# Two attentions of a hybrid decoder layer in one sequence of half-array passages

## The chip, the cores and the metric

The kernel runs on one core of a Trainium2 chip. The core has a matmul engine, TensorE (PE in the profile, with its weight loads in a lane of their own, PEld), a vector engine (VectorE, DVE), an activation engine (ScalarE, ACT), GpSimd (POOL) and SyncE (SP), whose queue issues nearly all transfers here. The metric is the time of one execution on the device in microseconds, less is better.

## The reference

Two decoder layers work on 256 tokens of width 1024. The input projection of a layer feeds three groups of heads; cut to what the change touches:

```python
proj = h @ w_in
q_r = rotary(split_heads(rq, RET_HEADS)); k_r = rotary(split_heads(rk, RET_HEADS)) * scale
y_ret = merge_heads(head_group_norm(retention(q_r, k_r, v_r))) * jax.nn.silu(rg)
y_moba = merge_heads(moba_attention(mq, mk, mv, rel_bias))     # causal softmax with a relative bias
y_conv = cb * causal_dwconv(cc * ch, conv_w)
mix = concatenate([y_ret, y_moba, y_conv], -1) @ w_out
x = layer_norm(DN_ALPHA * x + mix); x = layer_norm(DN_ALPHA * x + conv_ffn(x))
```

Six heads of 64 features do retention, six do MoBA attention, which at 256 tokens has one block and so is plain causal softmax attention. Retention weights the scores by a fixed decay per head, has no softmax, and is normalised per head behind its values.

## The kernel before

All weights are split into a rounded part and a remainder (`whi`, `wlo`, by ACT and DVE in `split`, lines 82 and 83), and most products are made of three matmuls, high by high, high by low and low by high. Tokens are two tiles of 128, and the features of two heads share the 128 partitions of one tile.

In each layer, ahead of the stretch that changes, PE makes the MoBA queries and keys (`feature_block`, lines 307 to 309). Then comes the stretch itself. Twelve projection blocks (retention queries and keys, `rq` and `rk`, three each, then six blocks of the short convolution) run through a generator, `projections`, and each is yielded in two halves of 12 full-array matmuls of 256 columns (lines 396 to 398). I call such a half a slice; `fill(n)` runs n of them. Between the slices the attentions are put by hand, one pair of heads at a time:

- `moba_scores(j)`: four products per head, one in plain fp32 and three of split parts, each head on one half of the 128 rows of the array (`Pair.scores`, line 335, the halves in `HALVES`). DVE adds the bias and takes the row minimum of the negated scores (445), ACT the exponential (447), DVE the reciprocal and the scaling (450, 452).
- `moba_transpose(j)`: six full-array transposes (459); ACT copies them back to SBUF (460).
- `moba_values(j)`: four products with 64 stationary columns, one head on each half of the columns (467); ACT and DVE split the result into `cath` and `catl`.
- `retention_scores(j)`: the same product as for MoBA (335); DVE multiplies by the decay (492, 493) into `rs`.
- `retention_values(h)`: three products per head with 128 queries as stationary columns and 64 features streamed (498 to 500), into the two banks `po`.

A plain fp32 matmul of the program shows as two matmuls and two weight loads in the trace. PE takes its work in the program's order. The loops put two or one slices between any two of these passages (`FILL`), so that scores wait through five slices for their transposes. All PSUM tiles come from two pools of four banks: `acc`, for the projections, and `att`, for the attentions, of which `po` holds two from the first retention scores to the head normalisation. The order on DVE and ACT is made by a scheduler when the program is built. SP fetches weights five blocks ahead.

```python
for i in range(NH // 2 + 2):
    if i < NH // 2: moba_scores(i)
    fill(FILL[0])
    if 0 <= i - 1 < NH // 2: moba_transpose(i - 1)
    fill(FILL[1])
    if 0 <= i - 2 < NH // 2: moba_values(i - 2)
```

Of the kernel before, what the change touches and what calls it, by code (L numbers as in the profile page):

```python
# [12 lines left out]
AF = mybir.ActivationFunctionType  # L13
# [3 lines left out]
P = 128  # L17
D = 1024
T = 256
# [3 lines left out]
NH = 6  # L23
# [17 lines left out]
TAIL = 4  # L41
LAST = 5
GSTEP = 3
FILL = (2, 1, 1, 2)
AT = ((7, 8), (7, 8), (6, 8), (13, 15))
WARM = 6
BIAS_AT = 6
# [1 line left out]
HALVES = (slice(0, HD), slice(HD, P))  # L49
# [3 lines left out]
def hybrid_decoder(ctx: ExitStack, tc: tile.TileContext, x, xw, wva, wvb, wf, wt, w_out, wg, w_up, w_down,  # L53
                   conv_w, ffn_w, ln1_g, ln1_b, ln2_g, ln2_b, rel_bias,
                   c_ident, c_rot, c_decay, c_bucket, out):
    nc = tc.nc
# [9 lines left out]
    def acc():  # L66
        return pa.tile([P, 512], F32, name="acc", tag="acc")

    def att():
        return pb.tile([P, 512], F32, name="att", tag="att")  # L70
# [10 lines left out]
    def split(dst_hi, dst_lo, src):  # L81
        nc.scalar.copy(dst_hi, src)  # L82
        nc.vector.tensor_sub(dst_lo, src, dst_hi.bitcast(F32))  # L83
# [141 lines left out]
    def mirrored(src, n):  # L225

        return bass.AP(tensor=src.tensor, offset=src.offset + P - 1, ap=[list(src.ap[0]), [P, n], [-1, P]])
# [31 lines left out]
    def fetch_table(func, after):  # L259

        nc.scalar.activation(sp.tile([P, 1], F32, name="table", tag="table", bufs=1), after[:, :1], func)
# [11 lines left out]
    for k in range(KD):  # L273
        hi, lo = weights(0, "v", k)
        for g in (1, 0):
            n, c = VG[g][1] - VG[g][0], slice(0, T) if g else slice(T, 3 * T)
# [12 lines left out]
    for l in range(DEPTH):  # L289
# [25 lines left out]
        rv = [v[:, HW:2 * HW] for v in vt]  # L315
# [21 lines left out]
        def buf256(name):  # L337
            return ap.tile([P, T], F32, name=name, tag="b256", bufs=3)

        moba = [Pair() for _ in range(3)]  # L340
        for i, m in enumerate(moba):
            p = feature_block(f"mq{i}")[:, :T]
            q = buf256("q")
# [86 lines left out]
        def fill(n):  # L430
            for _ in range(n):
                next(bulk, None)
# [3 lines left out]
        prob = {}  # L436

        def moba_scores(j):
            banks = [att(), att()]
            moba[j].scores(banks, slice(0, P), slice(P, 3 * P))  # L440
            for h, ps in zip((2 * j, 2 * j + 1), banks):
                m = sp.tile([P, 4], F32, name="sm", tag="sm")
                pr_ = prob[h] = ap.tile([P, HW], F32, name="prob", tag="t384", bufs=6)
                for t, s, bs in ((0, slice(0, P), slice(P, T)), (1, slice(P, 3 * P), slice(0, T))):
                    nc.vector.tensor_tensor_reduce(pr_[:, s], ps[:, s], bias[:, h, bs], -1.0, 3e38,
                                                   op0=ALU.add, op1=ALU.min, accum_out=m[:, t:t + 1])
                    nc.scalar.activation(pr_[:, s], pr_[:, s], AF.Exp, bias=m[:, t:t + 1], scale=-1.0,
                                         accum_out=m[:, 2 + t:3 + t])
                rs = sp.tile([P, 2], F32, name="rs", tag="rs")
                nc.vector.reciprocal(rs, m[:, 2:4])  # L450
                for t, s in ((0, slice(0, P)), (1, slice(P, 3 * P))):
                    nc.vector.tensor_scalar_mul(pr_[:, s], pr_[:, s], rs[:, t:t + 1])

        def moba_transpose(j):

            for h in (2 * j, 2 * j + 1):
                pt = att()
                for i in range(3):
                    nc.tensor.transpose(pt[:, i * P:i * P + P], prob[h][:, i * P:i * P + P], ident)
                nc.scalar.copy(prob[h].rearrange("p (t q) -> p t q", t=3), mirrored(pt[:, :HW], 3))  # L460

        def moba_values(j):

            po = att()
            for t, s in ((0, slice(0, T)), (1, slice(T, 3 * P))):
                for h, r in zip((2 * j, 2 * j + 1), HALVES):
                    nc.tensor.matmul(po[r, t * P:T], mv[t][:, h * HD:h * HD + HD], prob[h][:, s],
                                     start=t == 0, stop=t == 1)
            split(ch[:, 3 + j, :], cl[:, 3 + j, :], po[:, :T])

        for i in range(NH // 2 + 2):
            if i < NH // 2:
                moba_scores(i)
            fill(FILL[0])
            if 0 <= i - 1 < NH // 2:
                moba_transpose(i - 1)
            fill(FILL[1])
            if 0 <= i - 2 < NH // 2:
                moba_values(i - 2)

        fetch_table(AF.Silu, prob[NH - 1])


        po = [att(), att()]
        rs_ = {}

        def retention_scores(j):
            banks = [att(), att()]
            ret[j].scores(banks, slice(T, 3 * P), slice(0, T))
            for h, ps in zip((2 * j, 2 * j + 1), banks):  # L490
                s = rs_[h] = ap.tile([P, HW], F32, name="rs", tag="t384", bufs=6)
                nc.vector.tensor_mul(s[:, 0:T], ps[:, 0:T], decay[:, h, :])
                nc.vector.tensor_mul(s[:, T:3 * P], ps[:, T:3 * P], decay[:, h, 0:P])

        def retention_values(h):
            s = rs_[h]
            c = slice(h * HD, h * HD + HD)
            nc.tensor.matmul(po[0][:, c], s[:, 0:P], rv[0][:, c], start=True, stop=True)
            nc.tensor.matmul(po[1][:, c], s[:, P:T], rv[0][:, c], start=True, stop=False)
            nc.tensor.matmul(po[1][:, c], s[:, T:3 * P], rv[1][:, c], start=False, stop=True)  # L500

        for j in range(NH // 2 + 1):
            if j < NH // 2:
                while len(turned) <= j:
                    next(bulk)
                if j == 0:
                    fill(FILL[2])
                retention_scores(j)
            fill(FILL[3])
            if j:  # L510
                retention_values(2 * j - 2)
                retention_values(2 * j - 1)
        mvr = sp.tile([P, NT * NH, 2], F32, name="gmv", tag="gmv", bufs=1)
        for t in range(NT):
            st = sp.tile([P, NH, 6], F32, name="gst", tag="gst", bufs=2)
# [12 lines left out]
        for t, p in enumerate(token_group("rg")):  # L528
            c, g = slice(t * HW, t * HW + HW), slice(t * NH, t * NH + NH)
# [254 lines left out]
```

## Time and profile before

| | |
|---|---|
| median of 3 runs | 625.51 us (624.73 to 625.52) |
| the profiled execution | 625.28 us |
| its span, first to last instruction | 623.2 us |
| PE busy | 611.4 us, 98% |
| DVE busy | 456.9 us, 73% |
| ACT busy | 351.5 us, 56% |
| the stretch of the attentions, layer 0 and 1 | 49.31 and 48.93 us |

A row of the timeline gives the start and the time of one instruction, or of several of one kind in a row (x4). A matmul's time there includes its way through the array, so matmuls that follow each other overlap: their pace is the distance between starts. A passage's price is read as the distance from the matmul ahead of it to the one behind it.

### The profile page before, as it was taken

Reading aid. Unit: us, or ns where it says so; the run is one execution under the profiler, and the core shown is the slowest. Engines: PE = TensorE matmul, PEld = TensorE weight load, DVE = VectorE, ACT = ScalarE, POOL = GpSimd, SP = SyncE. Lnnn points to the kernel's source line nnn. Section 1 sums busy time; section 2 is a strip of 40 time slices with the busy share of each in tenths; the row PEclk is TensorE's granted clock in tenths of the full one; section 3 lists DMA queues with packets and bytes.
Section 4 is the critical chain, followed back from the end, with each engine's and each line's share of the span. In section 5 each row is a group of like instructions: output and inputs, shape, how many; then the busy total and the mean of one; then the engine's idle time right before and its main releaser. Section 6 shows DMA issues by size and latency. Waiting matters only on the chain.

```text
span 623.2 us, 10002 instructions
## 1 busy us (share of the span) xinstructions
PE 611.4 (98%) x3774; PEld 540.7 (87%) x3774; DVE 456.9 (73%) x834; ACT 351.5 (56%) x637; POOL 17.0 (3%) x18
## 2 busy tenths in 40 slices
PE   8999999999999999999999999999999999999994
PEld 6899998788888888899889999987888888888993
DVE  6478889777676777678765778888867676767846
ACT  6579837256556565566346794461655656556620
POOL 0100002000000000000000000101000000000001
PEclk9999999999999999999999999999999999999998
DMA  8987355546566556668327435473655555566501
GB/s 311 351 295 239 120 169 187 218 150 214 180 192 190 185 186 191 197 214 293 108 92 265 150 93 173 160 254 105 226 179 191 185 187 182 199 193 176 172 2 67
DMA packets 33675, 115.92 MB, mean 186 GB/s; under 512 B 3957, under 2 KB 4764, under 8 KB 33628
## 3 DMA queue, kind: packets, MB, share of 16 engines
q1 hardware_dynamic: 33356, 114.50, 56.3%
q0 software_dynamic: 272, 0.80, 0.4%
q8 instruction: 29, 0.48, 0.3%
q14 instruction: 18, 0.15, 0.1%
HBM read 114.22 MB, written 1.06 MB: 185 GB/s over the span
## 4 chain that ended last, share of the span: by engine, by line
PE 93%; DVE 4%; DMA 1%; POOL 0%; issue 0%; ACT 0%; SPq 0%; DVEq 0%; POOLq 0%
PE acc L632 18%; PE acc L633 9%; PE att L230 6%; PE att L231 6%; PE att L232 6%; PE acc L231 5%; PE acc L232 5%; PE acc L230 5%; PE acc L308 5%; PE acc L309 5%; PE acc L307 5%; PE acc L396 5%; PE acc L397 4%; PE acc L398 4%; PE att L335 2%; DVE st L240 1%
## 5 line engine op out<-in xcount | busy, mean ns | idle before, releaser
L83 DVE TENSOR_TENSOR wlo<-raw,whi 128x1024 fp32r<-128x1024 f32 (+3 forms) x207 | 229.5, 1115 | 87.5 <-ACT whi L82 86.6
L82 ACT CAST whi<-raw 128x1024 fp32r<-128x1024 f32 (+3 forms) x207 | 197.8, 963 | 114.0 <-PE acc L632 41.9
L632 PE MATMUL acc<-xx,whi 128*128 128x512 f32 x480 | 170.8, 398 | 0.0
L633 PE MATMUL acc<-xx,wlo 128*128 128x256 f32 x480 | 134.7, 281 | 0.0
L632 PEld LDWEIGHTS acc<-xx,whi 128*128 128x128 f32 x480 | 90.2, 188 | 22.0
L633 PEld LDWEIGHTS acc<-xx,wlo 128*128 128x128 f32 x480 | 90.6, 189 | 1.3
L308 PE MATMUL acc<-xx,whi 128*128 128x256 f32 x240 | 67.9, 283 | 0.0
L309 PE MATMUL acc<-xx,wlo 128*128 128x256 f32 x240 | 67.9, 283 | 0.0
L307 PE MATMUL acc<-xx,whi 128*128 128x256 f32 x240 | 67.9, 283 | 0.0
L396 PE MATMUL acc<-xx,whi 128*128 128x256 f32 x208 | 61.4, 295 | 0.0
L397 PE MATMUL acc<-xx,whi 128*128 128x256 f32 x208 | 58.7, 282 | 0.0
L398 PE MATMUL acc<-xx,wlo 128*128 128x256 f32 x208 | 58.7, 282 | 0.0
L231 PE MATMUL att<-whi,hl 128*128 128x512 f32 x144 | 56.5, 392 | 0.0
L232 PE MATMUL att<-wlo,hh 128*128 128x512 f32 x144 | 56.0, 389 | 0.0
L230 PE MATMUL att<-whi,hh 128*128 128x512 f32 x144 | 55.7, 394 | 0.0
L230 PE MATMUL acc<-whi,xx 128*128 128x512 f32 (+2 forms) x128 | 45.8, 362 | 1.5 <-ACT whi L82 1.5
L308 PEld LDWEIGHTS acc<-xx,whi 128*128 128x128 f32 x240 | 46.1, 192 | 0.2
L307 PEld LDWEIGHTS acc<-xx,whi 128*128 128x128 f32 x240 | 46.1, 192 | 0.2
L309 PEld LDWEIGHTS acc<-xx,wlo 128*128 128x128 f32 x240 | 46.1, 192 | 0.0
L231 PE MATMUL acc<-whi,xx 128*128 128x512 f32 (+2 forms) x128 | 44.9, 352 | 0.8 <-DVE xx L83 0.8
L232 PE MATMUL acc<-wlo,xx 128*128 128x512 f32 (+2 forms) x128 | 44.3, 350 | 0.0
L396 PEld LDWEIGHTS acc<-xx,whi 128*128 128x128 f32 x208 | 39.6, 190 | 2.7 <-issue 1.0
(141 smaller groups left out, 953.9 us busy)
## 6 DMA issues: line engine op xcount, KB each, us to landing
raw<-in_w_up_dram SPq DMA_DIRECT2D x80, 512.0 KB, 4.3
raw<-in_w_down_dram SPq DMA_DIRECT2D x44, 512.0 KB, 4.3
raw<-in_wf_dram SPq DMA_DIRECT2D x36, 512.0 KB, 4.6
raw<-in_w_out_dram SPq DMA_DIRECT2D x16, 512.0 KB, 3.4
raw<-in_wg_dram SPq DMA_DIRECT2D x8, 512.0 KB, 4.4
raw<-in_xw_dram SPq DMA_DIRECT2D x7, 512.0 KB, 5.7
raw<-in_wt_dram SPq DMA_DIRECT2D x8, 384.0 KB, 3.3
lnp<-in_ln_g_dram SPq DMA_DIRECT2D x4, 512.0 KB, 3.9
```

The lines of the kernel that those rows point to most:

```text
L82: nc.scalar.copy(dst_hi, src)
L83: nc.vector.tensor_sub(dst_lo, src, dst_hi.bitcast(F32))
L230: nc.tensor.matmul(ps, lhi, rhi, start=first, stop=False)
L231: nc.tensor.matmul(ps, llo, rhi, start=False, stop=False)
L232: nc.tensor.matmul(ps, lhi, rlo, start=False, stop=last)
L307: nc.tensor.matmul(ps[:, :T], hi[:, c], xh[:, k, :], start=k == 0, stop=False)
L308: nc.tensor.matmul(ps[:, :T], hi[:, c], xl[:, k, :], start=False, stop=False)
L309: nc.tensor.matmul(ps[:, :T], lo[:, c], xh[:, k, :], start=False, stop=k == KD - 1)
L396: nc.tensor.matmul(ps[:, :T], hi[:, c], xh[:, k, :], start=k == 0, stop=False)
L397: nc.tensor.matmul(ps[:, :T], hi[:, c], xl[:, k, :], start=False, stop=False)
L632: nc.tensor.matmul(ps, hi[:, c], xx[:, k].rearrange("p s t -> p (s t)"), start=k == 0, stop=False)
L633: nc.tensor.matmul(ps[:, T:], lo[:, c], xx[:, k, 0, :], start=False, stop=k == KD - 1)
```

## The change

The MoBA loop and the retention loop become one loop of five rounds. In a round the values of one pair, the scores of another, and in the last two rounds retention scores, stand directly behind each other; then come the transposes of the pair before, and then four slices. The retention values come after the loop, all six heads in one block, and the last four slices behind them. Their stationary columns are taken in halves of 64 queries, each on one half of the array's columns. `po` is allocated behind the loop, the MoBA values take an `acc` bank instead of an `att` bank, and ACT's table for Silu is fetched one round earlier.

```diff
-FILL = (2, 1, 1, 2)
+FILL = 4
...
         def moba_values(j):
 
-            po = att()
+            po = acc()
...
-        for i in range(NH // 2 + 2):
-            if i < NH // 2:
-                moba_scores(i)
-            fill(FILL[0])
-            if 0 <= i - 1 < NH // 2:
-                moba_transpose(i - 1)
-            fill(FILL[1])
-            if 0 <= i - 2 < NH // 2:
-                moba_values(i - 2)
-
-        fetch_table(AF.Silu, prob[NH - 1])
-
-
-        po = [att(), att()]
+
         rs_ = {}
...
         def retention_values(h):
+
             s = rs_[h]
             c = slice(h * HD, h * HD + HD)
-            nc.tensor.matmul(po[0][:, c], s[:, 0:P], rv[0][:, c], start=True, stop=True)
-            nc.tensor.matmul(po[1][:, c], s[:, P:T], rv[0][:, c], start=True, stop=False)
-            nc.tensor.matmul(po[1][:, c], s[:, T:3 * P], rv[1][:, c], start=False, stop=True)
-
-        for j in range(NH // 2 + 1):
-            if j < NH // 2:
+            for t, k, q in ((0, 0, 0), (1, 0, P), (1, 1, T)):
+                for r in HALVES:
+                    nc.tensor.matmul(po[t][r, c], s[:, q + r.start:q + r.stop], rv[k][:, c], start=k == 0, stop=k == t)
+
+
+        pairs = NH // 2
+        for i in range(pairs + 2):
+            if i >= 2:
+                moba_values(i - 2)
+            if i < pairs:
+                moba_scores(i)
+            for j in {pairs: (0,), pairs + 1: range(1, pairs)}.get(i, ()):
                 while len(turned) <= j:
                     next(bulk)
-                if j == 0:
-                    fill(FILL[2])
                 retention_scores(j)
-            fill(FILL[3])
-            if j:
-                retention_values(2 * j - 2)
-                retention_values(2 * j - 1)
+            if 0 < i <= pairs:
+                moba_transpose(i - 1)
+            if i == pairs:
+                fetch_table(AF.Silu, prob[NH - 1])
+            fill(FILL)
+        po = [att(), att()]
+        for h in range(NH):
+            retention_values(h)
```

On PE, the third scores of layer 0 stand between two slices in the program before:

```order
L398 MATMUL acc<-xx,wlo 128x256
L335 MATMUL att<-plain 128x128 x2
L335 MATMUL att<-pair 128x256 x6
L396 MATMUL acc<-xx,whi 128x256
L397 MATMUL acc<-xx,whi 128x256
```

and in the changed program behind the values of the first pair (467) and ahead of the transposes of the second (459):

```order
L398 MATMUL acc<-xx,wlo 128x256
L467 MATMUL acc<-prob,v 64x256 x2
L467 MATMUL acc<-prob,v 64x128 x2
L335 MATMUL att<-plain 128x128 x2
L335 MATMUL att<-pair 128x256 x6
L459 MATMUL att<-ident,prob 128x128 x6
L396 MATMUL acc<-xx,whi 128x256
```

Values, scores and transposes have moved together, with no slice between them.

On PE again, the retention values of one pair of heads in layer 0 before (`v_146` and `v_147` are the values of the two token tiles, `att_1010` and `att_1011` the banks `po`):

```order
L398 MATMUL acc_1158<-xx_78,wlo_890 128x256
L498 MATMUL att_1010<-v_146,rs_1091 128x64
L499 MATMUL att_1011<-v_146,rs_1091 128x64
L500 MATMUL att_1011<-v_147,rs_1091 128x64
L498 MATMUL att_1010<-v_146,rs_1094 128x64
L499 MATMUL att_1011<-v_146,rs_1094 128x64
L500 MATMUL att_1011<-v_147,rs_1094 128x64
L396 MATMUL acc_1201<-xx_78,whi_950 128x256
```

and the last head of the block of all six in the changed program:

```order
L488 MATMUL att_1144<-v_146,rs_1073 64x64 x2
L488 MATMUL att_1145<-v_146,rs_1073 64x64 x2
L488 MATMUL att_1145<-v_147,rs_1073 64x64 x2
L396 MATMUL acc_1219<-xx_78,whi_889 128x256
L397 MATMUL acc_1219<-xx_78,whi_889 128x256
```

Each product has become two with half the stationary columns, and the three blocks have become one.

On DVE, behind the scores of the first pair of layer 0 (`prob_572` is its head 1, `sw` and `a` belong to the rotary embedding of the slices), before:

```order
L83 TENSOR_TENSOR wlo_583<-raw_581,whi_582 128x1024
L450 RECIPROCAL rs_577<-sm_571 128x2
L445 ISA prob_655,sm_654<-att_644,bias_87 128x128
L445 ISA sm_654 128x1
L452 TENSOR_SCALAR prob_572<-prob_572,rs_577 128x128
L452 TENSOR_SCALAR prob_572<-prob_572,rs_577 128x256
```

and now:

```order
L83 TENSOR_TENSOR wlo_583<-raw_581,whi_582 128x1024
L450 RECIPROCAL rs_577<-sm_571 128x2
L387 TENSOR_TENSOR sw_612<-sw_612,rot_82 128x256
L452 TENSOR_SCALAR prob_572<-prob_572,rs_577 128x128
L452 TENSOR_SCALAR prob_572<-prob_572,rs_577 128x256
L388 TENSOR_TENSOR a_613<-acc_587,rot_82 128x256
```

The first step of the next pair's softmax (445) has moved behind, and a rotary product (387) stands ahead of the two scalings that complete head 1.

## Rows read from the trace of the kernel before

**Rows 1.** The page: busy time by engine, and the chain that ended last

```profile
PE 611.4 (98%) x3774; PEld 540.7 (87%) x3774; DVE 456.9 (73%) x834; ACT 351.5 (56%) x637; POOL 17.0 (3%) x18
...
PE 93%; DVE 4%; DMA 1%; POOL 0%; issue 0%; ACT 0%; SPq 0%; DVEq 0%; POOLq 0%
```

**Rows 2.** Windows: the attention stretches; busy us by engine, PE clock, DMA

```profile
41.27:90.58 49.31, 49.31 (x427) 46.48 (x427) 41.71 (x114) 38.10 (x90) 0.00 (x0) 1.00 0.57 184
346.83:395.76 48.93, 48.93 (x427) 46.19 (x427) 38.80 (x111) 36.14 (x88) 0.00 (x0) 1.00 0.42 130
```

**Rows 3.** PE's waits in the whole span: total us, times, longest

```profile
PE acc L230 <- ACT whi L82: 1.5, 2, 1.2
...
PE att L268 <- DVE x L254: 0.3, 1, 0.3
```

**Rows 4.** Timeline of PE around the first scores (start us, us)

```profile
41.07 0.28 PE L309 MATMUL acc<-xx,wlo 128*128 128x256 f32 x1
41.27 0.49 PE L335 MATMUL att<-plain 64*128 64x128 f32 x4
...
42.05 0.39 PE L396 MATMUL acc<-xx,whi 128*128 128x256 f32 x1
42.27 0.28 PE L397 MATMUL acc<-xx,whi 128*128 128x256 f32 x1
```

**Rows 5.** Timeline of PE around the first MoBA values

```profile
58.17 0.28 PE L398 MATMUL acc<-xx,wlo 128*128 128x256 f32 x1
...
59.40 0.28 PE L397 MATMUL acc<-xx,whi 128*128 128x256 f32 x1
```

**Rows 6.** Timeline of PE around the first transposes

```profile
50.17 0.28 PE L398 MATMUL acc<-xx,wlo 128*128 128x256 f32 x1
50.29 0.82 PE L459 MATMUL att<-ident,prob 128*128 128x128 f32 x6
...
51.07 0.28 PE L397 MATMUL acc<-xx,whi 128*128 128x256 f32 x1
```

**Rows 7.** Timeline of PE around the retention values of one pair

```profile
84.99 0.28 PE L398 MATMUL acc<-xx,wlo 128*128 128x256 f32 x1
85.11 0.33 PE L498 MATMUL att<-v,rs 128*128 128x64 f32 x2
85.28 0.39 PE L499 MATMUL att<-v,rs 128*128 128x64 f32 x2
...
86.57 0.28 PE L397 MATMUL acc<-xx,whi 128*128 128x256 f32 x1
```

**Rows 8.** Timeline of PE's weight loads, into first scores and first values

```profile
40.95 0.19 PEld L309 LDWEIGHTS acc<-xx,wlo 128*128 128x128 f32 x1
41.27 0.30 PEld L335 LDWEIGHTS att<-plain 64*128 64x128 f32 x4
41.49 0.42 PEld L335 LDWEIGHTS att<-pair 64*128 64x128 f32 x6
...
58.05 0.19 PEld L398 LDWEIGHTS acc<-xx,wlo 128*128 128x128 f32 x1
58.37 0.63 PEld L467 LDWEIGHTS att<-prob,v 128*64 128x64 f32 x8
```

**Rows 9.** Source view of line 467: ns min/median/max, first and last start

```profile
L467 PEld LDWEIGHTS att<-prob,v x48: 132/136/137, 58.4 to 375.7; 128*64 128x64 f32 x48
```

**Rows 10.** Timeline of PE at the third retention scores, layer 0

```profile
80.99 0.76 PE L335 MATMUL att<-plain 64*128 64x128 f32 x3
```

**Rows 11.** Timelines of ACT and DVE at the end of the first softmax

```profile
47.35 1.12 ACT L386 COPY sw<-acc 32x256 f32<-32x256 f32 x3
...
48.01 0.55 DVE L452 TENSOR_SCALAR prob<-prob,rs 128x128 f32<-128x128 f32 x2
48.50 0.43 DVE L387 TENSOR_TENSOR sw<-sw,rot 128x256 f32<-128x256 f32 x1
```

**Rows 12.** Timeline of ACT at the table load, layer 0

```profile
71.15 1.28 ACT L261 ACT_TABLE_LOAD   x1
```

## Prediction

> **What bounds the kernel now.** I began with the page's busy table and its chain that ended last: TensorE (PE) is busy 98% of the span and the chain runs 93% on it [rows 1]. An average of that kind says nothing of one stage, so I looked next at the two stretches from the first score matmul of a layer to the first matmul of the gate projection. In both, PE is busy for the whole stretch, 49.31 and 48.93 us, at full clock [rows 2]. VectorE (DVE) has 41.71 and 38.80 us of work there, so it has room, though not much in layer 0. The view of PE's waits has four rows in the whole run, from 1.5 us down to 0.3, none on a line of the attentions [rows 3]. So time is saved here only by shortening what PE itself does, and lost only by a wait that is not there now.
>
> Inside that stretch I read PE's timeline, row by row. A projection slice is 12 full-array matmuls 0.12 us apart; 24 slices make 34.56 us of either stretch, and the change leaves them alone. The rest is short passages. I price each as the distance from the last full matmul ahead of it to the second behind it, less two steps of 0.12:
> - a score passage (64-row tiles): 42.27 − 41.07 − 0.24 = 0.96 us [rows 4]
> - a MoBA value passage (64-column tiles): 59.40 − 58.17 − 0.24 = 0.99 us [rows 5]
> - six transposes: 51.07 − 50.17 − 0.24 = 0.66 us [rows 6]
> - the retention values of one head pair, 12 records: 86.57 − 84.99 − 0.24 = 1.34 us [rows 7], thus 36 records per layer at 0.11.
>
> A layer has 6 score passages (three MoBA, three retention) and three of each other kind: 5.76 + 2.97 + 1.98 + 4.02 = 14.73 us. With 34.56 that is 49.3, against 48.93 measured in layer 1, where the ends of the stretch are cut a little shorter.
>
> **What a switch costs.** The weight loads show where a passage's time goes. Full-array loads stand 0.12 apart. Into a score passage the gap is 41.27 − 40.95 = 0.32, into a value passage 58.37 − 58.05 = 0.32: some 0.20 extra each [rows 8]. Inside a score passage two pairs of loads take 41.49 − 41.27 = 0.22, so five pairs are 0.55 of its 0.96 us, and entering and leaving together take 0.41. The same 0.41 leaves 0.58 for the work of a value passage. Transposes follow a full matmul after the ordinary 0.12 [rows 6]: they run in the full array and cost no switch.
>
> **The change, part by part.**
>
> *Passages joined.* Per layer, two score passages stay alone (1.92 us), the transposes stay (1.98), two passages become MoBA values plus one score block (0.58 + 0.55 + 0.41 + x each, 3.08 + 2x), and one becomes values plus two score blocks (0.58 + 1.10 + 0.41 + x = 2.09 + x). x is the price of going from 64-column tiles straight to 64-row tiles, and no row shows such a step. From above I bound it by a full entry, 0.20, from below by zero (the step from one score pair to the next, already counted, is the cheapest change of tile there is; nothing suggests a gain). I take 0.20, since both entries from the full array cost that whichever way the array was halved. The Trainium skill, "TensorEngine Tiling (Array Packing)", section Tiling Modes, Key Properties, says that changing the tiling mode, not just the tile, drains the engine. The 0.32 us load gaps agree for full to half, no run here shows half to half; by that rule x is a whole switch, and by the joining alone three x of 0.20 per layer would be saved besides.
>
> *Retention values in halves.* 36 full-width records at 0.11 us become 72, two abreast on 64 columns each, in a passage of their own: 36w + 0.41. w is the time of one pair of records, not in the trace. Now the loads set the pace: the first two matmuls of a block, whose loads lie ahead of it, take only 85.28 − 85.11 = 0.17, so one of them takes about 0.06, the others 0.11 [rows 7]. Eight 64-column loads of a value passage, 136 ns each in the median, go through in 0.63 us, so they overlap [rows 8, 9]. From below: a value passage streams 256 + 256 + 128 + 128 = 768 columns in 0.58 us, so 64 columns take 0.048. From above: 0.11, no gain. I take 0.06, the row of a matmul with the same 64 columns. 36 × 0.06 = 2.16.
>
> Together, after: 1.92 + 1.98 + 3.08 + 2.09 + 0.41 + 3 × 0.20 + 2.16 = 12.24 us, against 14.73: **2.49 us saved per layer**, 4.98 in two.
>
> *Waits that go.* In layer 0 PE stands in the third retention score block until DVE's L493 has emptied a bank: its first three plain records take 0.76 us, where all four take 0.49 elsewhere [rows 4, 10]. In layer 1 that gap is missing, and the stretches differ by 49.31 − 48.93 = 0.38 us [rows 2]. The output pair `po` no longer holds two of the four `att` banks through the retention, so this wait goes: −0.38.
>
> *Waits that may come.* The scores of pair i now have four slices (5.76 us) and the next score passage ahead of their transposes, where they had five slices. In layer 0 the order of DVE puts L387 ahead of head 1's two L452. L387 needs the copies of L386, done at 47.35 + 1.12 = 48.47, so L452 starts at about 48.85 and ends at 49.40, where it ended at 48.56 [rows 11]. PE gets there earlier: the 48th slice matmul at 42.27 + 46 × 0.12 = 47.79, scores from 48.00, transposes from 48.77, head 1's at about 49.2. I charge 0.2 us. The same walk, with DVE's and ACT's own order and durations like these, leaves 0.9 us or more at the other transposes of layer 0 and 1 to 2 us in layer 1; the values of pair 1 in layer 0 have only 0.1, for which I charge 0.1. Behind a transpose that waits stand the slices, and nothing else gets in.
>
> *Answers that are plain.* MoBA values move to an `acc` bank, needed again two joined passages and four slices later, some 10 us, longer than its split needs. ACT's table load of 1.28 us [rows 12] now stands ahead of the split of the last key block; by my walk the third retention scores still find that split done 0.5 us early; with that cover gone the load would cost PE up to its 1.28 us in a layer. Head statistics start four slices earlier, with POOL's one rsqrt behind them. SP's queue keeps its order. These I cost at nothing: slices cover them.
>
> **The sum.** −4.98 − 0.38 + 0.30 = −5.06. The profiled execution took 625.28 us (a span of 623.2 and 2.1 around it); that makes 620.2. The median of the runs is 0.23 higher, so I give **620.4 us**.
>
> **Rivals.**
>
> *The inner step is free* (x = 0): 1.2 us less in two layers, 619.2. For it: nothing is loaded for the full array in between. Against it: both entries cost alike. With w = 0.048 as well, another 0.9, 618.3.
>
> *The retention halves cannot be fed.* 72 matmuls and 72 loads in some 2.2 us means a matmul every 30 ns. The densest stretch in the trace is the inside of a score passage, ten records in 0.55 us, 0.055 each [rows 4, 8]. If that is the pace at which PE can be handed work, a pair keeps 0.11, the values stay at about 4.0 us and pay their switch besides: (0.11 − 0.06) × 36 = 1.8 worse per layer, 624.0. For it: every passage today is short and stands behind slow slices, which let work pile up ahead. Against: those 0.055 are what the loads of 128 columns take there, so they show no pace of issue. The Trainium skill, "TensorE: Matmul & The Clock Gate", section "Wait — 56ns, not 53.3ns?", states some 62 ns of sequencer time per matmul where hardware decoding is off; by it the block would take 72 × 0.062 = 4.5 us, an estimate from that page, and the rows so far allow either.
>
> *Transposes wait for the softmax: slower than before.* Place: the six transpose blocks, each behind its own scores by four slices where there were five. Latency from scores to normalised probabilities was 48.56 − 42.05 = 6.5 us for pair 0 [rows 4, 11], and PE now comes 48.77 − 42.05 = 6.7 after them. DVE takes its work in order, so one late copy on ACT moves all of it. It decides from 5.06 / 6 = 0.85 us at each block; at 1.2 us each the time is 620.4 + 7.2 = 627.6. Against it: the walk finds one wait, of 0.2.
>
> *It doesn't do what it says*: score blocks behind values wait for a bank or for turned keys, and PE drains anyway, 0.8 us at three places per layer: 625.2.
>
> **How the numbers follow.** Forecast 0.58 (619.6 to 621.5), free inner step 0.12, unfed halves 0.16 (623 to 625), waiting transposes 0.09 (621 to 628), undone joining 0.05. A measurement tells 0.2%, 1.25 us, from no change. Faster by that: 0.70 from the first two, 0.08, 0.05 and 0.02 from the others, 0.85. Within: 0.07 + 0.01 + 0.02 = 0.10. Slower: 0.05, by waiting transposes above all. The range runs from 618.3, both unknown prices at their low ends, to 624.2, halves without gain; about 0.15 lies outside.
>
> **What the profile of after would show.** Right: stretches of 46.4 to 46.8 us; loads 0.32 apart at 12 entries or exits between full and half and about as far between values and scores; pairs of retention values near 0.06; PE waits on L452 in layer 0 only, 0.2 or so. Wrong: a pair at 0.11 or more, an inner gap near 0.12, or waits on L452 or L460 of more than 0.5 each.

## The result, and the profile after

The changed kernel takes 620.88 us (median of four runs, 620.47 to 621.64), against 625.51 before; the ratio is 0.9931, with a 95% interval from 0.9915 to 0.9947. The profiled execution took 620.47 us. Its span shrank from 623.2 to 618.7 us, by 4.5; 0.3 more lies outside the span.

The page of the changed kernel, busy time by engine and the chain that ended last, answers to [rows 1]:

```profile
PE 607.8 (98%) x3846; PEld 536.7 (87%) x3846; DVE 456.2 (74%) x834; ACT 351.9 (57%) x637; POOL 15.4 (2%) x18
...
PE 83%; DVE 7%; ACT 4%; DMA 2%; issue 1%; POOL 0%; SPq 0%; DVEq 0%; ACTq 0%; POOLq 0%
```

PE has 72 records more (3,846 for 3,774) and 3.6 us less to do. It is still busy 98%, but the chain runs on PE for 83% where it was 93%: other engines hold PE up in more places. The windows of the two attention stretches, with the columns of [rows 2], say how much came from there:

```profile
41.05:88.36 47.31, 47.31 (x464) 44.35 (x464) 40.81 (x133) 36.66 (x88) 2.02 (x1) 1.00 0.57 181
344.71:391.20 46.49, 46.49 (x463) 44.15 (x463) 38.77 (x130) 35.07 (x86) 1.95 (x1) 1.00 0.41 126
```

Layer 0 lost 2.00 us and layer 1 lost 2.44, at full clock in both. In layer 1 the starts of matmuls show no wait, before or after, so it is the clean measurement: 2.44 where 2.49 were expected. PE's waits in the whole span, to be held against [rows 3]:

```profile
PE att L180 <- DVE zero L177: 1.1, 1, 1.1
PE acc L231 <- DVE xx L83: 0.7, 3, 0.2
PE acc L230 <- ACT whi L82: 0.7, 2, 0.4
PE att L268 <- DVE gate L532: 0.4, 1, 0.4
```

The last row is new and lies behind the stretch, where nothing was expected. This view lists no wait on a line of the attentions, since it counts an engine as busy while a matmul is on its way; the small waits there are read from the distances between starts.

**The two unknown prices.** PE's timeline of the changed kernel around the block of retention values:

```profile
80.04 0.28 PE L398 MATMUL acc<-xx,wlo 128*128 128x256 f32 x1
80.25 2.32 PE L488 MATMUL att<-v,rs 128*64 128x64 f32 x72
82.50 0.39 PE L396 MATMUL acc<-xx,whi 128*128 128x256 f32 x1
82.72 0.28 PE L397 MATMUL acc<-xx,whi 128*128 128x256 f32 x1
```

By the method of [rows 7] the block costs 82.72 − 80.04 − 0.24 = 2.44 us. The first and the last of its 72 records start 2.10 us apart: 0.058 for a pair, 0.029 for a record on average. And around the second scores, which stand directly behind values:

```profile
55.34 0.87 PE L467 MATMUL acc<-prob,v 128*64 128x256 f32 x8
56.14 0.49 PE L335 MATMUL att<-plain 64*128 64x128 f32 x4
```

From the first value matmul to what follows it takes 0.80 us. One of the experiments below puts a slice there, and the slice starts 0.80 behind the values too. So going from 64-column tiles to 64-row tiles takes as long as going back to the full array. The weight loads say the same: the last of the values starts at 55.83, the first of the scores at 56.14, a gap of 0.31 where an entry from the full array has 0.32 [rows 8].

**Where the waits came.** The first transposes and the values of the second pair, in layer 0:

```profile
48.54 1.12 PE L459 MATMUL att<-ident,prob 128*128 128x128 f32 x6
49.41 0.36 PE L396 MATMUL acc<-xx,whi 128*128 128x256 f32 x1
...
63.47 1.43 PE L467 MATMUL acc<-prob,v 128*64 128x256 f32 x8
64.83 0.49 PE L335 MATMUL att<-plain 64*128 64x128 f32 x4
```

Six transposes behind scores take 0.63 us elsewhere and 49.41 − 48.54 = 0.87 here, a wait of 0.24. DVE completes their head 1 meanwhile, behind L387, which had waited for ACT's L386 as the prediction walked it:

```profile
48.62 0.54 DVE L452 TENSOR_SCALAR prob<-prob,rs 128x128 f32<-128x128 f32 x2
```

Values take 0.80 elsewhere and 64.83 − 63.47 = 1.36 here, a wait of 0.56. ACT's timeline shows what the values wait for:

```profile
62.00 0.51 ACT L447 ACTIVATE prob<-prob,sm 128x256 f32<-128x256 f32 x1
...
62.51 0.39 ACT L447 ACTIVATE prob<-prob,sm 128x128 f32<-128x128 f32 x1
...
62.90 0.49 ACT L447 ACTIVATE prob<-prob,sm 128x256 f32<-128x256 f32 x1
...
63.51 0.48 ACT L460 COPY prob<-att 128x384 f32<-128x384 f32 x1
```

The copy of the second head's transposes stands on ACT behind three exponentials of the next pair and ends at 63.99, half a microsecond after PE came for it; PE's load for that head starts at 64.04.

**Behind the stretch.** The gate is transposed by L268 among the matmuls of the output projection. Before, all six transposes stood behind six of these matmuls:

```profile
98.99 0.39 PE L230 MATMUL acc<-whi,cath 128*128 128x512 f32 x1
...
100.38 0.81 PE L268 MATMUL att<-ident,gate 128*128 128x128 f32 x6
```

In the changed kernel three of them stand behind the first one, and PE waits there:

```profile
96.68 0.40 PE L230 MATMUL acc<-whi,cath 128*128 128x512 f32 x1
97.47 0.55 PE L268 MATMUL att<-ident,gate 128*128 128x128 f32 x3 [0.39 <-DVE gate L532]
```

From the first of these matmuls to the first one on `hhi` it is 11.57 us before (98.99 to 110.57) and 12.24 after (96.68 to 108.92); in layer 1 it is 11.57 and 11.75. DVE's and ACT's timelines say why the gate is late although the values of the retention, which it needs, come earlier:

```profile
90.92 0.55 DVE L528 TENSOR_TENSOR yn<-att,gmv 128x384 f32<-128x384 f32 x1
...
91.72 2.35 DVE L83 TENSOR_TENSOR wlo<-raw,whi 128x1024 fp32r<-128x1024 f32 x2
...
94.33 0.55 DVE L530 TENSOR_TENSOR yn<-yn,grstd 128x384 f32<-128x384 f32 x1
...
95.26 1.21 DVE L83 TENSOR_TENSOR wlo<-raw,whi 128x1024 fp32r<-128x1024 f32 x1
96.39 0.55 DVE L530 TENSOR_TENSOR yn<-yn,grstd 128x384 f32<-128x384 f32 x1
96.86 0.55 DVE L532 TENSOR_TENSOR gate<-gate,yn 128x384 f32<-128x384 f32 x1
```

```profile
95.84 0.49 ACT L531 ACTIVATE gate<-acc 128x384 f32<-128x384 f32 x1 [2.19 <-PE acc L232]
```

The few steps of the gate are spread over 6.5 us among conversions of weights, and the product ends at 97.41, just ahead of the transposes. The product also needs ACT's Silu of the gate projection, which waits for PE and ends at 96.33. So even with an idle DVE it could have started 0.53 us earlier and no more, however early the values of the retention come. In layer 1 the product is done at 399.77 and the transposes start at 399.83, only 0.07 later than without a wait. The scheduler, which I had told of for DVE and ACT alone, orders PE's queue as well, so PE does not always take its work in the program's order: in layer 0 the transposes were set ahead of the time at which DVE's queue has the gate. Why it chose so isn't in the trace.

**The whole difference**, from the starts of matmuls in the two traces:

| | expected | measured |
|---|---|---|
| layer 1, stretch | −2.49 | −2.44 |
| layer 0, stretch | −2.57 | −2.00 |
| output projection, layer 0 and 1 | 0 | +0.67, +0.18 |
| wait of L268 for x in layer 0 [rows 3] | 0 | −0.49 |
| ahead of the first scores | 0 | −0.22 |
| gate projections | 0 | −0.16 |
| sum | −5.06 | −4.46 |

The wait on x of [rows 3] cost 0.49 between starts of matmuls; it is absent from the other kernels' traces below too, even from the one with the order of before, so I don't count it as the change's. The time ahead of the first scores, where weights first arrive, differs by up to 1.8 us among the profiled runs below. The 0.16 does belong to the change: the gate projection takes 8.41 us to 8.43 in the traces where the retention values stand directly ahead of it, and 8.33 where slices stand between, so a part of the price of the retention values had fallen behind the stretch.

### The profile page after: what moved, and what is told of

The parts are those of the page before. It is cut to its first block, busy times and chain, and to the rows that moved or that the text cites. A ratio compares the mean times of both kernels' runs of the same rounds, so it can differ in the third digit from the quotient of the medians.

```text
span 618.7 us, 10157 instructions
## 1 busy us (share of the span) xinstructions
PE 607.8 (98%) x3846; PEld 536.7 (87%) x3846; DVE 456.2 (74%) x834; ACT 351.9 (57%) x637; POOL 15.4 (2%) x18
## 4 chain that ended last, share of the span: by engine, by line
PE 83%; DVE 7%; ACT 4%; DMA 2%; issue 1%; POOL 0%; SPq 0%; DVEq 0%; ACTq 0%; POOLq 0%
PE acc L628 18%; PE acc L629 9%; PE att L230 6%; PE att L231 6%; PE att L232 6%; PE acc L308 5%; PE acc L309 5%; PE acc L307 5%; PE acc L231 4%; PE acc L232 4%; PE acc L230 4%; PE acc L396 3%; PE acc L397 2%; PE acc L398 2%; DVE wlo L83 2%
```

## The experiments

### One part at a time

**The halves undone.** The changed kernel with full-width retention values:

```diff
-            for t, k, q in ((0, 0, 0), (1, 0, P), (1, 1, T)):
-                for r in HALVES:
-                    nc.tensor.matmul(po[t][r, c], s[:, q + r.start:q + r.stop], rv[k][:, c], start=k == 0, stop=k == t)
+            nc.tensor.matmul(po[0][:, c], s[:, 0:P], rv[0][:, c], start=True, stop=True)
+            nc.tensor.matmul(po[1][:, c], s[:, P:T], rv[0][:, c], start=True, stop=False)
+            nc.tensor.matmul(po[1][:, c], s[:, T:3 * P], rv[1][:, c], start=False, stop=True)
```

> The changed kernel with the retention values taken at full width again, so one part of the change is undone. The theory prices a pair of half-width value matmuls at 0.058 us and a full-width record at 0.11, with two switches of 0.20 around the halves alone: the block of all six heads grows from the 2.44 us of the changed kernel's trace to about 4.0, +1.6 per layer, +3.2 in all, so 624.1 us, with pairs gone and records 0.11 apart. The rival, that the whole gain came from joining the passages and from the waits that left, and that the halves gain no more than their switches cost, expects 620.9, no change.

It took 623.78 us, ratio to before 0.9978 (0.9969 to 0.9987). PE's timeline at the block:

```profile
80.43 0.28 PE L398 MATMUL acc<-xx,wlo 128*128 128x256 f32 x1
80.55 0.33 PE L486 MATMUL att<-v,rs 128*128 128x64 f32 x2
...
84.69 0.28 PE L397 MATMUL acc<-xx,whi 128*128 128x256 f32 x1
```

The block costs 84.69 − 80.43 − 0.24 = 4.02, and 2.44 in halves: 1.58 per layer, as the theory had it. The stretches are 48.86 and 48.07 us, 1.55 and 1.58 longer. The rival's 620.9 lies outside the interval. The medians differ by 2.90 only, since the output projection of layer 0 takes 11.74 us here and 12.24 in the changed kernel. Three gate transposes stand behind its first matmul here too, but DVE has run ahead: it waits 0.68 us for ACT's Silu and completes the product 0.25 us behind that matmul, where the changed kernel has 0.73. By this trace, of the 0.67 lost there 0.17 goes with the place, as in layer 1, and 0.50 with DVE's queue.

**The halves alone.** The kernel before with the same six products in its three passages per layer (the diff above, turned round).

> The kernel before with the retention values in halves of 64 queries and nothing else changed, so the halves stand in three passages per layer. The theory: each passage is 12 pairs at 0.058 us and two switches, 0.70 + 0.41 = 1.11 us against 1.34, so 0.23 less at six places, 1.4 us in all, and perhaps up to 0.2 more per layer where scores follow directly: 623.7 to 624.1 us. If the switches cost nothing at these short passages the passages would take 0.70, 3.8 us less in all, 621.7. If half-width matmuls are slower to issue when a passage is short, the time is 625.5 or above.

It took 623.70 us, ratio 0.9980 (0.9970 to 0.9989), at the favourable end of the theory's 623.7 to 624.1. PE's timeline at two of the passages in layer 1:

```profile
384.48 0.92 PE L500 MATMUL att<-v,rs 128*64 128x64 f32 x24
385.33 0.49 PE L335 MATMUL att<-plain 64*128 64x128 f32 x4
...
388.96 0.28 PE L398 MATMUL acc<-xx,wlo 128*128 128x256 f32 x1
389.17 0.92 PE L500 MATMUL att<-v,rs 128*64 128x64 f32 x24
390.02 0.39 PE L396 MATMUL acc<-xx,whi 128*128 128x256 f32 x1
390.24 0.28 PE L397 MATMUL acc<-xx,whi 128*128 128x256 f32 x1
```

and behind the first of them in layer 0:

```profile
80.92 0.90 PE L335 MATMUL att<-plain 64*128 64x128 f32 x3 [0.22 <-DVE rs L493]
```

The lone passage costs 390.24 − 388.96 − 0.24 = 1.04 us; 1.11 was expected, and 1.34 is the price at full width [rows 7]. Twelve pairs are 0.70 of it, so entering and leaving together take 0.34, not 0.41. The block of 72 records says the same: 2.44 less 36 pairs at 0.058 leaves 0.35. Layer 1 is 1.05 us shorter than before: three times 0.30, and 0.15 at the one place where scores follow directly. Halves in short passages give 1.05 us in layer 1, and one passage instead of three gives the rest of the 1.58. Layer 0 got only 0.61. There the values and the scores behind them take 2.43 us (79.79 to 82.22) and 1.63 in layer 1, so 0.81 is a wait on L493, where the kernel before has 0.38: PE comes earlier for the same product of DVE. The agreement of the whole time is thus partly luck: the passages gain 0.4 us more than expected, and the wait takes as much.

**The joining undone.** Two of the four slices moved in between values and scores:

```diff
             if i >= 2:
                 moba_values(i - 2)
+                fill(FILL // 2)
...
-            fill(FILL)
+            fill(FILL // 2 if i >= 2 else FILL)
```

> The changed kernel with two of the four slices moved in between the MoBA values and the scores that followed them directly, in three rounds per layer, so the joining is undone and the halves stay. The theory prices the inner step at one switch of 0.20 us, and leaving plus entering again at 0.41: 0.21 more at six places, 1.2 us, so 622.1, with waits on the softmax moved by a few tenths either way. The rival, that going from 64-column tiles to 64-row tiles is free and the gap of 0.20 there is something else, expects 0.41 at six places, 2.5 us, 623.4. If the joining is worth nothing: 620.9.

It took 621.93 us, ratio 0.9948 (0.9936 to 0.9961): 1.05 above the changed kernel, near the 1.2 of the theory, but the intervals overlap. The sum hides more than it shows, so I read one place. From the first values to the second, the changed kernel needs 63.47 − 55.34 = 8.13 us and this one 8.30, with the same work in between:

```profile
55.34 0.87 PE L467 MATMUL acc<-prob,v 128*64 128x256 f32 x8
56.14 0.39 PE L396 MATMUL acc<-xx,whi 128*128 128x256 f32 x1
...
63.64 1.10 PE L467 MATMUL acc<-prob,v 128*64 128x256 f32 x8
...
367.26 1.25 PE L467 MATMUL acc<-prob,v 128*64 128x256 f32 x8 [0.33 <-ACT prob L460]
```

So a joint is worth 0.17 us here, and 0.19 at the third place, some 1.1 at six places. The theory's 0.21 is near, the free step's 0.41 is out, and so is a joint worth nothing. But waits moved as well: the second values of layer 0 wait 0.23 where it was 0.56, the third now wait 0.17, and those of the second pair in layer 1 now wait for their ACT copies (last row), by 0.8 in all. That is 0.6 more, and the output projection of layer 0, where the transposes of the gate happen to stand better, gives 0.5 back. The agreement of the whole time is partly luck, that of the place is not.

### The waits that came

**The gate later.** All six gate transposes are held behind the twelve matmuls of the first output weight tile:

```diff
-            transpose_split(t, gt, ch, cl, 3, 0)
...
-                    out_mm(t, h, hi, lo, ch[:, k, :], cl[:, k, :], n == 0, False)
+                    done = out_mm(t, h, hi, lo, ch[:, k, :], cl[:, k, :], n == 0, False)
+            if n == 0:
+                with tc.issue_after(done.ins):
+                    for t in range(NT):
+                        transpose_split(t, gate[:, t * HW:t * HW + HW], ch, cl, 3, 0)
```

> The changed kernel with the six gate transposes of both token tiles held behind the twelve out-projection matmuls of the first weight tile, where three of them stand behind the first such matmul. The theory: the changed kernel's PE waits there for the gate of DVE, 0.7 us in layer 0 and 0.3 in layer 1, and behind twelve matmuls the gate is done, so 0.6 to 1.0 us less, 620.0 to 620.3 us. The rival, that the time is lost again because the transposes' output is then needed before it is there, or because DVE is as late as its queue makes it, expects 620.9.

It took 620.37 us, just above the range, ratio 0.9925 (0.9912 to 0.9937): an interval that overlaps the changed kernel's, so the times don't tell them apart. The trace does. From the first of these matmuls to the first on `hhi` it takes 11.63 us in either layer, 0.61 and 0.12 less than the changed kernel, and the wait on L532 is gone. In the profiled run 0.53 of that was lost ahead of the first scores (41.58 us instead of 41.05), where this edit changes nothing.

**More slices.** Five slices in the first and third rounds:

```diff
-FILL = 4
+FILL = (5, 4, 5, 4, 4)
...
-            fill(FILL)
+            fill(FILL[i])
```

> The changed kernel with five slices instead of four in the first and third round of either layer, and two instead of four behind the retention values; nothing else is changed. In the changed kernel PE waits 0.24 us at the first transposes and 0.56 at the values of the second pair in layer 0. The theory, that both wait for a softmax result which DVE and ACT finish a little after PE gets there, expects both waits gone with 1.44 us more ahead of them, 0.8 us less: 620.1 us, if the gate, now with two slices of cover, makes PE wait no longer than it does. The rival, that these waits sit in the order of ACT and DVE, which the scheduler fits to PE, expects waits of the same size elsewhere and 620.9 or more. A gate that comes later by the two slices would cost up to 2.9 us, and the time would be above 622.

It took 619.11 us, ratio 0.9899 (0.9885 to 0.9912), which is faster than the changed kernel and 1.0 below the expectation. The windows of the stretches:

```profile
41.09:87.59 46.50, 46.50 (x464) 44.16 (x463) 42.44 (x133) 36.85 (x88) 0.00 (x0) 1.00 0.60 195
343.30:389.81 46.51, 46.51 (x464) 44.16 (x464) 39.56 (x130) 35.23 (x86) 0.00 (x0) 1.00 0.44 136
```

Both waits of layer 0 are gone, 47.31 − 46.50 = 0.81 us, and no other took their place: both layers now have the stretch that layer 1 has in the changed kernel. The rest came from the gate, against my fear for it with only two slices of cover:

```profile
96.38 0.49 PE L268 MATMUL att<-ident,gate 128*128 128x128 f32 x3
...
98.32 0.52 PE L268 MATMUL att<-ident,gate 128*128 128x128 f32 x3
```

The scheduler put the first three transposes behind two matmuls and the others behind eight, and PE waits at neither; the output projection takes 11.65 us. A retention block that ends 2.1 us later (84.61 for 82.50) gave a gate that is waited for less. So the time at which the values come does not decide. Two things do: the place of the transposes, which alone was changed in the run before this, and DVE's queue, which here completes the first product at 96.19, 0.27 behind the first matmul of the output projection.

> The kernel with five, four, five, four and four slices and, besides, the six gate transposes held behind the first twelve out-projection matmuls. If the two savings add, 0.8 us at the transposes and values of layer 0 and 0.5 to 0.9 at the gate, it takes 619.2 to 619.6 us. If the gate is late because only two slices stand behind the retention values, it waits behind the twelve matmuls too, and the time is 620.4 or more.

Both edits together: 619.17 us, ratio 0.9900 (0.9887 to 0.9914). They don't add, since more slices had already put the gate right; both take some 11.6 us there.

### Fewer passages

**Four passages per layer** should save two passages and one inner step. The loop gives way to a list, with seven, four, six, four and three slices, and the gate's transposes are held as above:

```diff
+        moba_scores(0)
+        moba_scores(1)
+        fill(FILL[0])
+        moba_transpose(0)
+        moba_transpose(1)
+        fill(FILL[1])
+        moba_values(0)
+        moba_values(1)
+        moba_scores(2)
+        retention_scores(0)
+        fill(FILL[2])
+        moba_transpose(2)
+        fetch_table(AF.Silu, prob[NH - 1])
+        fill(FILL[3])
+        moba_values(2)
+        retention_scores(1)
+        retention_scores(2)
+        fill(FILL[4])
+        po = values_of_retention()
```

> A version meant to be faster than both: per layer the first two MoBA score blocks directly behind each other, their transposes seven slices later, the values of both pairs and two score blocks in one passage, and the gate transposes held behind twelve out-projection matmuls. Two half-array passages and one inner step fewer per layer save 2 x 0.41 + 0.20 = 1.02 us by the theory, 2.0 in all, on top of 0.5 to 0.9 at the gate and 0.8 for the waits of layer 0: 617.2 to 617.6 us. The rival: the softmax of two pairs at once keeps DVE and ACT past the seven slices, and the single MoBA pair behind them past its six, so PE waits for transposes or values by 0.5 us or more at some places, and the time is 618.5 to 620.5.

It took 624.17 us, ratio 0.9982 (0.9973 to 0.9991), and neither expectation holds. PE's waits and the place in layer 0:

```profile
PE acc L467 <- DVE a L388: 3.5, 3, 1.5
PE att L268 <- DVE gate L539: 1.4, 2, 1.0
```

```profile
61.31 0.49 PE L335 MATMUL att<-plain 64*128 64x128 f32 x4
...
63.91 0.87 PE L467 MATMUL acc<-prob,v 128*64 128x256 f32 x8 [1.54 <-DVE a L388]
```

The softmax of two pairs was in time. What was missing is a bank: two value tiles want two banks of the projections' pool at once, and one is held until DVE's rotary product L388 has read it. In layer 0 the scheduler put the second values among the scores, which adds switches. Besides, no slice stands behind the retention values, and the gate is waited for.

**One bank for both pairs.** Each pair needs 256 of a bank's 512 columns:

```diff
-            po = acc()
...
-        moba_values(0)
-        moba_values(1)
+        both = acc()
+        moba_values(0, both[:, :T])
+        moba_values(1, both[:, T:])
```

> The kernel of four passages with one edit: the MoBA values of the first two pairs share one bank of the projections' pool (256 columns each) where each took its own. The theory: that kernel is slow because PE stands in its values until DVE's L388 has emptied a bank that the second pair's values need; in its trace the two value blocks and the scores between and behind them take 1.7 us longer in either layer than their own work. With one bank those 3.4 us go: 620.7 us, the waits at the gate staying. The rival, that PE there waits for the softmax of two pairs, which a bank does not change, expects 624.

> Four passages per layer with the shared bank, slices seven, four, five, four and three between them and one behind the retention values, the gate transposes where the scheduler puts them. The theory expects stretches of 45.5 us in both layers, 1.0 shorter than with more slices, so 617.1 us, if the gate has the cover that one slice and the gate projection give; the rival, that the gate is late without slices behind the retention values, as in the kernel of four passages (1.4 us of waits), expects 618.0 to 618.6.

> As the one before, with six slices instead of seven behind the first scores and two instead of one behind the retention values. By the theory of the passages 617.1 us too, with less wait at the gate; the rival is that the transposes of the first two pairs, 8.6 us behind the second pair's scores, come before DVE has scaled four heads: then PE waits there by 0.5 us or more in a layer and the time is 618 or more.

They took 629.15 us (ratio 1.0062, 1.0049 to 1.0075), 628.93 (1.0056, 1.0038 to 1.0074) and 627.80 (1.0037, 1.0023 to 1.0052): slower than the kernel before. My theory had the bank right and the remedy wrong. The last of the three, in PE's timeline of layer 0:

```profile
64.39 0.87 PE L465 MATMUL acc<-prob,v 128*64 128x256 f32 x8 [2.47 <-DVE catl L83]
```

The second pair's values now wait (2.5 us here, 3.9 in layer 1) until DVE has read the first pair's half. That is not the whole loss. After these stands PE's granted clock fell to 0.50, the lower of its two levels (1.2 GHz), as the window from 66 to 69 us shows (columns as in [rows 2]):

```profile
66.00:69.00 3.00, 3.00 (x16) 3.00 (x15) 2.48 (x11) 2.87 (x10) 0.00 (x0) 0.50 0.02 5
```

The matmuls of the slices stand 0.21 us apart there instead of 0.12. The stretches are 50.10 and 52.36 us, 4.2 and 6.5 longer than in the next kernel, which has the same slices: the waits are 2.5 and 3.9 of it, and most of the rest is the lower clock. The columns don't overlap, but the program keeps a write behind the reads of the whole tile. The Trainium skill, "PSUM — Partial Sum Buffer", section "PSUM bank collisions raise a hardware error", says that this wait belongs there: PE's write must be kept from another engine's read by bank and quadrant, not by address. No run here shows such a collision.

**Both values, then both splits.**

```diff
-            split(ch[:, 3 + j, :], cl[:, 3 + j, :], po[:, :T])
+            return lambda: split(ch[:, 3 + j, :], cl[:, 3 + j, :], po[:, :T])
...
-        moba_values(0, both[:, :T])
-        moba_values(1, both[:, T:])
+        for done in [moba_values(0, both[:, :T]), moba_values(1, both[:, T:])]:
+            done()
```

> The kernel of four passages, six, four, five, four and three slices and the shared bank, but with the split of the first two pairs' values behind the second pair's matmuls. The three kernels with a shared bank lost their time because the second pair's values waited for DVE's L83 to read the first pair's half of the tile, and the scheduler put them among scores or slices meanwhile. Theory: with both value blocks directly behind each other no such wait is there, each layer has 1.0 us less than the kernel with more slices (619.1), and the time is 617.1 us, if transposes and gate wait no more than in the kernel before this, where they did not. The rival, that the values of two pairs, one behind the other, wait for ACT's copies of four heads or for a bank by 1 us or more in each layer, expects 619 or more.

It took 618.16 us, ratio 0.9889 (0.9873 to 0.9906), the lowest median of all; its interval overlaps that of more slices. The windows:

```profile
42.60:88.48 45.88, 45.88 (x464) 44.08 (x463) 42.09 (x133) 37.27 (x88) 0.00 (x0) 1.00 0.60 197
344.18:390.01 45.83, 45.83 (x464) 44.05 (x464) 39.06 (x130) 35.37 (x86) 0.00 (x0) 1.00 0.44 138
```

The wait is gone, the clock stays at 1.00, and both stretches are 0.6 to 0.7 us shorter than with more slices, but not 1.0. A part is a small wait at the transposes of the third pair, 0.16 us in layer 0 and 0.11 in layer 1. Another is that transposes directly behind scores make a part of the exit free: scores, transposes and the return to slices cost 1.57 us in one (in the kernel with more slices 0.77, 0.63, and 0.17 for entry and return), where 0.96 + 0.66 = 1.62 stands for the two apart [rows 4, 6]. This order gives that up at three places per layer, 0.15. What is left of the gap, under 0.1, is not explained.

## Why the prediction was right, point by point

**The bound.** PE does set the time: what the passages lost came out of the stretch of layer 1 to within 0.05 us, though DVE has as much to do as before.

**The halves.** A pair was taken at 0.06 and measured 0.058, near the bound of 0.048 rather than 0.11. This also decides the rival of the halves that can't be fed: 72 matmuls went through 0.029 us apart on average, so its 0.055 per record was not the pace at which PE takes work. That it was the pace of loads of 128 columns, as the argument against it said, fits but was not tested. The 62 ns of the Trainium skill, "TensorE: Matmul & The Clock Gate", section "Wait — 56ns, not 53.3ns?", which the page ties to a decoding mode, does not hold in this kernel. The block's two switches were taken at 0.41 together and measured 0.35, so it costs 2.44 and not 2.57.

**The inner step.** Taken at 0.20. The values need 0.80 us to whatever stands behind them, scores or a slice, and opening a joint costs 0.17 to 0.19. The free step is out. The rule of the Trainium skill, "TensorEngine Tiling (Array Packing)", section Tiling Modes, Key Properties, that a change of the tiling mode drains the engine, now has a row for half to half as well.

**The wait that goes.** The third retention scores of layer 0 no longer wait for L493. With the halves alone, where the pair `po` still holds its banks, they still do, by 0.81 us.

**The waits that come.** The transposes were charged 0.2 and took 0.24, on the heads' L452 as foretold. The values of the second pair were charged 0.1 and took 0.56: this is the one term of the sum that was mis-sized. The walk had left 0.1 us of room at this place; against PE, the copy, which stands behind three exponentials, came more than half a microsecond later than the walk had it. A room of 0.1 us is more than such a walk can promise. By the prediction's own signs this one is wrong, a wait on L460 of more than 0.5 us, and the stretch of layer 0, 47.31, lies outside its 46.4 to 46.8. The rival of the waiting transposes is out even so: it asked for 0.85 us at each of six blocks, and one block waits, by 0.24. More slices ahead of both places removed both waits, 0.81 us for 0.80.

**The answers at nothing.** "Head statistics start four slices earlier ... slices cover them" failed. The statistics were early, but the gate also hangs on DVE's queue and on ACT's Silu, and the scheduler moved the gate's transposes forward on PE by more than these allowed: +0.67 and +0.18, of which some 0.17 in each layer goes with the place and 0.50 in layer 0 with DVE's queue. The kernel with more slices shows that another order has no such cost; holding them later shows it too. The table load and the `acc` bank of the values cost nothing, as said.

**The whole.** 5.06 us were expected and 4.46 measured in the span, and the median is 0.5 above the forecast: 0.46 for the values and 0.85 for the gate against it; 0.49, 0.22 and 0.16 for it, from places that the prediction did not treat, and only the last of them can be put down to the change. The whole is closer than its parts, and that is luck; the mechanism, cheaper passages on PE, is not.

## What to carry to other kernels

Price every change of tile shape on PE from the distances between matmul starts, and put passages with half-array tiles next to each other; a narrow product in two halves pays when its passage is long enough to spread the two switches (12 pairs gain 0.30 us, 36 gain 1.58). Then look at what the new order does on the other engines' queues: here one more slice at two places of a layer, taken from its end, brought 1.8 us between the medians, over a third of what the change itself brought. When two results share a PSUM tile, write both before either is read.

## What the runs showed of the hardware that I had not expected

TensorE takes matmuls of 64 columns, each with a weight load of its own, at 0.029 us apiece on average, on alternate halves, for 72 in a row (0.058 for a pair), where the full-width record of the same work takes 0.11 us. Entering and leaving the half array takes 0.34 to 0.35 us together around these products, a little less than the 0.41 around scores. After PE had stood for 2.47 us and for 3.92 in one kernel, its granted clock fell to 0.50, and matmuls stood 0.21 us apart where they stand 0.12 apart at full clock: a long wait cost more than itself.
